# Streaming the columns of every split-precision matmul in a woven order, with staggered weight slots

## The chip, the cores and the metric

The kernel runs on one core of one Trainium2 chip, as one launch. The time is device microseconds (us) of that core. A profiled execution gives a trace beside it; its span is the time from the first to the last instruction.

## The reference, cut to what matters

The input is one sequence of 256 tokens of width 1024, in float32. Five stages follow one another on the residual stream h, each behind an RMS norm: a gated feed-forward block, a mixer (a linear recurrence, windowed attention, and their projections), a second feed-forward block, and two layers of another hybrid kind (a convolution, a low-rank attention, a dilated attention in three groups, and gated output products).

```python
def swiglu(x, w_gu, w_down):                       # D_FF = 2816
    g, u = jnp.split(x @ w_gu, 2, axis=-1)
    return (jax.nn.silu(g) * u) @ w_down
...
    h = x
    f = swiglu(rms_norm(h, ffn1_pre_g), ffn1_w_gu, ffn1_w_down)
    h = h + 0.5 * rms_norm(f, ffn1_post_g)
    m = hybrid_mixer(rms_norm(h, mix_pre_g), ...)    # z = u @ w_in, ..., merged @ w_out
    h = h + rms_norm(m, mix_post_g)
    f = swiglu(rms_norm(h, ffn2_pre_g), ffn2_w_gu, ffn2_w_down)
    h = h + 0.5 * rms_norm(f, ffn2_post_g)
    for l in range(2):
        h = hybrid_layer(h, ..., w_in_2[l], ..., w_o_2[l])   # proj = h @ w_in, ..., x + merged @ w_o
```

Nearly all of the arithmetic is products of the 256 tokens with weight matrices that are read from HBM once, 227 MB in all.

## The kernel before, in words

Every large product is done in split precision. A float32 operand is written as the sum of two numbers of the type fp32r, hi and lo, and a product of two operands is three matmuls that add up in one PSUM tile: hi by hi, hi by lo, lo by hi. That is `mm3` (lines 221 to 225; its three matmuls are lines 223, 224 and 225, and all big groups of the trace carry these lines). A matmul holds a stationary operand of 128x128, which a weight load (PEld in the profile) puts into the array, and streams the columns of a moving operand past it.

The activations lie transposed in two tiles, xh and xl, of 8 x 256 columns (8 groups of 128 features, 256 tokens each). Weights come in units: `unit` starts one transfer into a slot of pool `raw` (four slots), and `split_raw` makes hi from it by a copy on ScalarE (line 206) and lo by a subtraction on VectorE (line 207), both in one slot of pool `w`. Pool w has NW = 8 slots of 8192 bytes in each partition, used in turn; hi and lo of a unit lie in one slot. A few units at the end of a stage go to slots of other pools (w2, b4, s) so that they can be loaded ahead.

There are two ways round in which a product uses them:

- `stepA`, `down` and `out_proj`: the tokens are the stationary operand (128 of them by 128 features) and the weights move, 512, 416 or 384 columns at a time. These are the groups ga, ua, q, kv, c, dqk, uq, ukv, dn and o.
- `pairB`: 128 columns of weights are the stationary operand and the 256 tokens move. These are gu, gp, xg, g, bz, cx, zb and po.

A feed-forward block walks over 11 pairs of 256 hidden columns: gu products of one pair, then the dn products of the pair before; the units of the last three pairs lie in pool w2, and their dn products come at the end. Mixer and layers run such products while small jobs (transposes, attention scores, values) are let in between the matmuls by `tick`, which keeps its own account of time.

The pools lie in each partition in the order of their making: constants, raw, w, small tiles, then b4, n, t, then xh and xl, then the pools of the stage. `softplus` (called once, from `params`, during the first feed-forward block) makes eight constants of 32 bytes, of which two are needed later; pool `t` is a turning pool of four scratch slots that the activations of the gu products use as well.

Of the kernel before, what the change touches and what calls it, by code (L numbers as in the profile page):

```python
# [10 lines left out]
F32 = mybir.dt.float32  # L11
F32R = mybir.dt.float32r
# [4 lines left out]
P = 128  # L17
# [4 lines left out]
NW = 8  # L22
# [60 lines left out]
CW = CONST.shape[1] - 512  # L83


def rows(x):
    return lambda k: (x[0][:, k], x[1][:, k])


class Job:  # L90
# [3 lines left out]
    def __init__(self, gen, ready):  # L94
        self.gen, self.ready, self.done = gen, ready, False


class Kern:
    def __init__(self, tc, a, ex):
        self.tc, self.nc, self.a = tc, tc.nc, a  # L100
        pool = lambda name, bufs, **kw: ex.enter_context(tc.tile_pool(name=name, bufs=bufs, **kw))
        self.const = pool("const", 1)
        self.rawp = pool("raw", NRAW)
        self.wp = pool("w", NW)
        self.sm = pool("sm", 6)
        self.pools = {n: pool(n, k) for n, k in (("b4", NB4), ("n", NN), ("t", NT))}
        self.xp = pool("xT", 1)
        self.psum = pool("ps", 1, space=PSUM)
        self.now, self.live, self.last = 0.0, 0, None
        self.taken = deque([-W_X] * NX)  # L110
        self.lanes = {n: deque() for n in ("tp", "T", "S")}

# [85 lines left out]
    def split_raw(self, raw, kt, cols, pool="w"):  # L198
        nc = self.nc
        if pool in ("w", "w2"):  # L200
            p = self.wp if pool == "w" else self.pools[pool]
            w = p.tile([P, 2, kt, cols], F32R, tag=pool, name=pool)
            hi, lo = w[:, 0], w[:, 1]
        else:
            hi, lo = (self.tl(pool, [P, kt, cols], "w" + pool, F32R) for _ in range(2))
        nc.scalar.copy(hi, raw)  # L206
        nc.vector.tensor_tensor(lo, raw, hi, op=ALU.subtract)  # L207
        return hi, lo
# [11 lines left out]

    def mm3(self, out, ah, al, bh, bl, first, last):
        m = self.nc.tensor.matmul
        m(out, lhsT=ah, rhs=bh, start=first, stop=False)  # L223
        m(out, lhsT=ah, rhs=bl, start=False, stop=False)  # L224
        self.last = m(out, lhsT=al, rhs=bh, start=False, stop=last).ins  # L225
# [104 lines left out]
    def softplus(self):  # L330

        nc = self.nc
        T = lambda n: self.const.tile([P, 8], F32, name=n)
        ts, tt, stt = nc.vector.tensor_scalar, nc.vector.tensor_tensor, nc.vector.scalar_tensor_tensor
        neg, absl, t, e, z, z2, s = (T(f"sp{i}") for i in range(7))
        ts(neg, self.lam, -1.0, None, op0=ALU.mult)
        tt(absl, neg, self.lam, op=ALU.max)
        nc.scalar.activation(t, absl, AF.Tanh, scale=1.0 / 32)
        ts(z, t, 1.0, None, op0=ALU.add)
        nc.vector.reciprocal(z, z)  # L340
        ts(e, t, -1.0, 1.0, op0=ALU.mult, op1=ALU.add)
        tt(e, e, z, op=ALU.mult)
        for _ in range(4):
            tt(e, e, e, op=ALU.mult)
        ts(z, e, 2.0, None, op0=ALU.add)
        nc.vector.reciprocal(z, z)
        tt(z, e, z, op=ALU.mult)
        tt(z2, z, z, op=ALU.mult)
        nc.vector.memset(s, 1.0 / 17)
        for n in (15, 13, 11, 9, 7, 5, 3, 1):  # L350
            tt(s, s, z2, op=ALU.mult)
            ts(s, s, 1.0 / n, None, op0=ALU.add)
        tt(s, s, z, op=ALU.mult)
        ts(neg, neg, 0.0, None, op0=ALU.max)
        self.sp2, self.nsp4 = T("sp2"), T("nsp4")
        ts(s, s, 4.0, None, op0=ALU.mult)
        stt(self.sp2, in0=neg, scalar=2.0, in1=s, op0=ALU.mult, op1=ALU.add)
        ts(self.nsp4, self.sp2, -2.0, None, op0=ALU.mult)
# [128 lines left out]
    def transposed(self, parts, take, name, rows=P):  # L487

        yield from self.room()
        ps = self.bank("x", name, (P, len(parts), P))  # L490
        for i, x in enumerate(parts):
            self.nc.tensor.transpose(ps[0:rows, i], x, self.id)
        take(ps[0:rows])
        yield 0.107 * len(parts), W_TP
# [73 lines left out]
    def mixer(self, xT):  # L568
# [37 lines left out]
        def gate(c0, f, th):  # L606
            col = c0 + f * 512
            banks = self.pairB(rows(xT), [w[:, col:col + 256], w[:, col + 256:col + 512]], "g", tags=("accB", "accB"))
            for j in range(2):
                nc.scalar.activation(th[j], banks[j], AF.Tanh, scale=0.5)  # L610
# [100 lines left out]
    def heads(self, pairs, v, mask, scale, emit, deps, out, sinks=None):  # L711
# [39 lines left out]
        def values():  # L751
            for m in range(len(pairs)):
                while len(ready) <= m or self.now < ready[m][1]:
                    yield 0.0, 0.3
                s = ready[m][0]
                yp = self.bank("yp", "yT", (P, S))
                pts = []
                for j in range(2):
                    yield from self.room()
                    pts.append(self.prob_T([s[:, j, b * P:(b + 1) * P] for b in range(3)]))  # L760
                    yield 0.32, W_T
                self.live -= 1
                self.pv_pair(yp, v[m], pts, True, True)
                emit(m, yp)
                yield 1.1, 0.0

        self.spawn("S", scores())
        out.append(self.spawn("T", values()))

# [420 lines left out]
class DilPair:  # L1190
# [46 lines left out]
    def attend(self, sz, yc, out):  # L1237
# [6 lines left out]
        def scores():  # L1244
            yield from k.after(*self.jobs)
            mx, nm, rs = (k.small([P, 2, 2], x) for x in ("dmx", "dnm", "drs"))
            sm = k.small([P, 2, 2, 3], "dsm")
            ss = []
            for g in range(3):
                s = yield from k.s_tile(2)  # L1250
                ss.append(s)
                yield from k.room(2)
                ps = k.score_pair([(qd[r, g], kd[r, g]) for r in rows])
                for j in range(2):
                    for t, c, dc in sides:
                        nc.vector.tensor_tensor_reduce(
                            s[:, j, c], in0=ps[j][:, c], in1=k.dist[:, g, dc], scale=-SLOPES[8 * g + 2 * m + j],
                            scalar=-3e38 if g == 0 else mx[:, j, t:t + 1], op0=ALU.add, op1=ALU.max, accum_out=mx[:, j, t:t + 1])
                yield 1.1, W_SC
            nc.vector.tensor_scalar(nm, mx, -1.0, None, op0=ALU.mult)  # L1260
            for g, s in enumerate(ss):
                for j in range(2):
                    for t, c, _ in sides:
                        nc.scalar.activation(s[:, j, c], s[:, j, c], AF.Exp, bias=nm[:, j, t:t + 1], accum_out=sm[:, j, t, g:g + 1])
            nc.vector.tensor_reduce(rs, sm, axis=mybir.AxisListType.X, op=ALU.add)
            nc.vector.reciprocal(rs, rs)
            for s in ss:
                for j in range(2):
                    for t, c, _ in sides:
                        nc.vector.tensor_scalar(s[:, j, c], s[:, j, c], rs[:, j, t:t + 1], None, op0=ALU.mult)  # L1270
            ready.append((ss, k.now + W_SD))

        def values():
            if not yc:
                yc.extend([k.b4([P, 4, S], "ych", F32R), k.b4([P, 4, S], "ycl", F32R)])
            while not ready or k.now < ready[0][1]:
                yield 0.0, 0.3
            yp = k.bank("yp", "dyT", (P, S))
            for g, s in enumerate(ready[0][0]):
                pts = []  # L1280
                for j in range(2):
                    yield from k.room()
                    pts.append(k.prob_T([s[:, j, b * P:(b + 1) * P] for b in range(3)]))
                    yield 0.32, W_T
                k.live -= 1
                k.pv_pair(yp, [[vd[:, b, (2 * g + j) * 64:(2 * g + j + 1) * 64] for b in range(2)] for j in range(2)], pts, g == 0, g == 2)
                yield 1.1, 0.0
            k.gated(yc, sz, m, yp)
            yield 0.64, 0.0

        k.spawn("S", scores())
        out.append(k.spawn("T", values()))

# [32 lines left out]
```

## Time and profile before

| | |
|---|---|
| time, median of 2 runs | 1368.24 us (1367.99 to 1368.49) |
| profiled execution | 1368.98 us |
| its span | 1367.2 us |
| PE, weight loads, VectorE, ScalarE busy | 98%, 90%, 69%, 57% of the span |
| read from HBM | 227.64 MB, 167 GB/s over the span with what is written |

The spans of matmuls in the trace overlap: a matmul's end is modelled, so its pace is read from the distance between the starts of neighbours, not from its duration.

### The profile page before, as it was taken

To read this page: it belongs to the slowest core of one execution; us is meant where nothing else is said; L and a number is where in the kernel's file an instruction comes from. 1 tells how busy PE (TensorE), PEld (TensorE's weight loads), DVE (VectorE), ACT (ScalarE), POOL (GpSimd) and SP (SyncE) were. 2 spreads that over 40 slices of the span, in tenths; PEclk is the share of its full clock that TensorE was granted. 3 is DMA by queue.
4 is the path that set the end of the run, shared out by engine and by line. 5 is a ranking of instruction groups with operands and counts; after the bars stand their busy time and mean duration, and the time that the engine had idled before them with its cause. 6 is when DMAs were issued, how large, how long until landed. Compare 5 with 4: busy or idle time off the path is not lost.

```text
span 1367.2 us, 24721 instructions
## 1 busy us (share of the span) xinstructions
PE 1339.2 (98%) x9434; PEld 1236.1 (90%) x9434; DVE 950.1 (69%) x2178; ACT 780.5 (57%) x1464; POOL 3.0 (0%) x10
## 2 busy tenths in 40 slices
PE   7999999999999999999999999999999999999998
PEld 5999987888998899998998989999889989899997
DVE  6546667887878655558888676665788886766663
ACT  6444544787754544444667776454546667755451
POOL 0000000000000000000000000000000000000000
PEclk9999999999999999999999999999999999999999
DMA  7657764436565565673754454656556553556661
GB/s 257 220 165 226 227 210 150 122 115 156 166 207 183 176 192 186 201 229 86 218 139 123 129 170 124 184 172 187 174 160 176 150 133 96 174 157 178 186 183 49
DMA packets 234807, 230.30 MB, mean 168 GB/s; under 512 B 12336, under 2 KB 213184, under 8 KB 234688
## 3 DMA queue, kind: packets, MB, share of 16 engines
q1 hardware_dynamic: 232432, 227.05, 55.7%
q10 hardware_dynamic: 2256, 1.67, 0.5%
q8 instruction: 74, 1.21, 0.4%
q14 instruction: 45, 0.37, 0.1%
HBM read 227.64 MB, written 1.05 MB: 167 GB/s over the span
## 4 chain that ended last, share of the span: by engine, by line
PE 83%; DVE 8%; ACT 4%; DMA 3%; issue 2%; SPq 0%; ACTq 0%; DVEq 0%
PE gu L225 5%; PE gu L223 5%; PE gu L224 5%; PE dqk L223 4%; PE dqk L225 4%; PE dqk L224 4%; PE gp L223 3%; PE gp L225 3%; PE gp L224 3%; PE dn L223 3%; PE dn L225 3%; PE dn L224 3%; PE po L223 2%; PE po L225 2%; PE po L224 2%; PE sc L791 2%
## 5 line engine op out<-in xcount | busy, mean ns | idle before, releaser
L207 DVE TENSOR_TENSOR w<-raw,w 128x1024 fp32r<-128x1024 f32 (+1 forms) x437 | 502.4, 1157 | 234.1 <-ACT w L206 232.4
L206 ACT CAST w<-raw 128x1024 fp32r<-128x1024 f32 (+1 forms) x437 | 432.8, 999 | 348.6 <-PE gu L225 53.6
L223 PE MATMUL gu<-xh,w 128*128 128x256 f32 x576 | 161.4, 280 | 0.0
L225 PE MATMUL gu<-xh,w 128*128 128x256 f32 x576 | 161.1, 280 | 0.0
L224 PE MATMUL gu<-xl,w 128*128 128x256 f32 x576 | 160.7, 279 | 0.0
L223 PE MATMUL dqk<-w,xh 128*128 128x384 f32 x384 | 136.7, 356 | 3.0 <-ACT sq L1023 3.0
L224 PE MATMUL dqk<-w,xh 128*128 128x384 f32 x384 | 129.7, 338 | 0.0
L225 PE MATMUL dqk<-w,xl 128*128 128x384 f32 x384 | 129.3, 337 | 0.0
L223 PE MATMUL gp<-xh,w 128*128 128x256 f32 x384 | 109.2, 285 | 0.0
L224 PEld LDWEIGHTS gu<-xl,w 128*128 128x128 f32 x576 | 108.0, 188 | 0.7
L223 PEld LDWEIGHTS gu<-xh,w 128*128 128x128 f32 x576 | 107.9, 187 | 0.7
L225 PEld LDWEIGHTS gu<-xh,w 128*128 128x128 f32 x576 | 108.2, 188 | 0.0
L224 PE MATMUL gp<-xl,w 128*128 128x256 f32 x384 | 107.2, 279 | 0.0
L225 PE MATMUL gp<-xh,w 128*128 128x256 f32 x384 | 107.1, 280 | 0.0
L223 PEld LDWEIGHTS dqk<-w,xh 128*128 128x128 f32 x384 | 72.1, 188 | 9.9 <-issue 6.0
L223 PEld LDWEIGHTS gp<-xh,w 128*128 128x128 f32 x384 | 72.0, 187 | 3.1 <-issue 2.7
L224 PEld LDWEIGHTS dqk<-w,xh 128*128 128x128 f32 x384 | 72.3, 188 | 0.2
L224 PEld LDWEIGHTS gp<-xl,w 128*128 128x128 f32 x384 | 72.2, 188 | 0.0
L225 PEld LDWEIGHTS dqk<-w,xl 128*128 128x128 f32 x384 | 72.1, 188 | 0.0
L225 PEld LDWEIGHTS gp<-xh,w 128*128 128x128 f32 x384 | 71.9, 188 | 0.0
L223 PE MATMUL dn<-w,aT 128*128 128x512 f32 x176 | 69.2, 393 | 0.0
L224 PE MATMUL dn<-w,aT 128*128 128x512 f32 x176 | 69.2, 393 | 0.0
(377 smaller groups left out, 3245.8 us busy)
## 6 DMA issues: line engine op xcount, KB each, us to landing
raw<-in_w_in_dram SPq DMA_DIRECT2D x140, 512.0 KB
raw<-in_ffn_w_gu_dram SPq DMA_DIRECT2D x88, 512.0 KB
raw<-in_w_in_dram SPq DMA_DIRECT2D x192, 192.0 KB
raw<-in_ffn_w_down_dram SPq DMA_DIRECT2D x44, 512.0 KB
raw<-in_w_o_dram SPq DMA_DIRECT2D x16, 512.0 KB
raw<-in_w_proj_attn_dram SPq DMA_DIRECT2D x16, 256.0 KB
raw<-in_w_proj_lru_dram SPq DMA_DIRECT2D x8, 512.0 KB
raw<-in_w_out_dram SPq DMA_DIRECT2D x8, 512.0 KB
```

The source lines that it names most:

```text
L206: nc.scalar.copy(hi, raw)
L207: nc.vector.tensor_tensor(lo, raw, hi, op=ALU.subtract)
L223: m(out, lhsT=ah, rhs=bh, start=first, stop=False)
L224: m(out, lhsT=ah, rhs=bl, start=False, stop=False)
L225: self.last = m(out, lhsT=al, rhs=bh, start=False, stop=last).ins
L791: self.nc.tensor.matmul(p[:, c], lhsT=q[:, cq], rhs=k[:, ck], start=True, stop=True)
```

## The change

`mm3` rearranges the moving operand and the output alike. Where the number of columns is a multiple of 128 (256, 384 and 512; not 416), the columns are taken 16 of the first half, 16 of the second half, the next 16 of the first half, and so on. Each column of the output still gets the product of its own column, so the tiles hold what they held before; only the order of streaming differs. Pool w gets one slot of its own name for each of the eight places, in the same rotation, with a tile of 64 bytes behind each slot that nothing uses; a slot is thus 8256 bytes from the next, and the eight begin 64 bytes apart mod 512. To have room, the seven scratch tiles of softplus become parts of one tile of pool t, and its two results get names of their own.

```diff
+def weave(x):
+    return x if x.shape[1] % 128 else x.rearrange("p (h a c) -> p a h c", h=2, c=16)
...
-        self.wp = pool("w", NW)
+        self.wp = pool("w", 1)
+        self.nw = 0
...
         if pool in ("w", "w2"):
-            p = self.wp if pool == "w" else self.pools[pool]
-            w = p.tile([P, 2, kt, cols], F32R, tag=pool, name=pool)
+            if pool == "w":
+                i = self.nw % NW
+                w = self.wp.tile([P, 2, kt, cols], F32R, tag=f"w{i}", name="w")
+                if self.nw < NW:
+                    self.wp.tile([P, 16], F32, tag=f"pad{i}", name=f"pad{i}")
+                self.nw += 1
+            else:
+                w = self.pools[pool].tile([P, 2, kt, cols], F32R, tag=pool, name=pool)
...
     def mm3(self, out, ah, al, bh, bl, first, last):
         m = self.nc.tensor.matmul
+        out, bh, bl = weave(out), weave(bh), weave(bl)
         m(out, lhsT=ah, rhs=bh, start=first, stop=False)
...
     def softplus(self):
         nc = self.nc
-        T = lambda n: self.const.tile([P, 8], F32, name=n)
+        scr = self.t([P, 7, 8], "sp")
+        T = lambda n: scr[:, int(n[2])] if n[2:].isdigit() else self.const.tile([P, 8], F32, name=n)
...
-        self.sp2, self.nsp4 = T("sp2"), T("nsp4")
+        self.sp2, self.nsp4 = T("spp"), T("nsp")
```

## Rows read from the trace of the kernel before

**Rows 1.** The page: busy time of each engine, and the chain by engine.
```profile
PE 1339.2 (98%) x9434; PEld 1236.1 (90%) x9434; DVE 950.1 (69%) x2178; ACT 780.5 (57%) x1464; POOL 3.0 (0%) x10
...
PE 83%; DVE 8%; ACT 4%; DMA 3%; issue 2%; SPq 0%; ACTq 0%; DVEq 0%
```

**Rows 2.** Windows: length, PE, PEld, DVE, ACT, POOL busy, clock, DMA share, GB/s.
```profile
0.00:50.00 50.00, 39.81 (x213) 33.00 (x214) 32.97 (x55) 29.31 (x40) 0.70 (x6) 1.00 0.80 261
...
241.00:463.00 222.00, 216.44 (x1589) 196.19 (x1588) 176.46 (x385) 152.11 (x293) 1.27 (x2) 1.00 0.51 154
```

**Rows 3.** Timeline of PE (start, duration), gate-up products; 20 rows left out.
```profile
104.05 0.28 PE L223 MATMUL gu<-xh,w 128*128 128x256 f32 x1
...
106.52 0.28 PE L223 MATMUL gu<-xh,w 128*128 128x256 f32 x1
```

**Rows 4.** Timeline of the weight loads at the same place.
```profile
104.05 0.19 PEld L224 LDWEIGHTS gu<-xl,w 128*128 128x128 f32 x1
```

**Rows 5.** Timeline of PE, gate products of the mixer, two stretches.
```profile
290.54 0.28 PE L224 MATMUL g<-xl,w 128*128 128x256 f32 x1
...
292.35 0.28 PE L225 MATMUL g<-xh,w 128*128 128x256 f32 x1
...
293.78 0.28 PE L224 MATMUL g<-xl,w 128*128 128x256 f32 x1
...
294.96 0.28 PE L225 MATMUL g<-xh,w 128*128 128x256 f32 x1
```

**Rows 6.** Windows of these two stretches, columns as in rows 2.
```profile
290.54:292.35 1.81, 1.81 (x18) 1.81 (x17) 1.24 (x2) 1.30 (x4) 0.00 (x0) 1.00 1.04 348
293.78:294.96 1.18, 1.18 (x13) 1.18 (x11) 1.18 (x4) 1.18 (x4) 0.00 (x0) 1.00 0.88 305
```

**Rows 7.** Timeline of PE, the end of the first down product.
```profile
192.00 0.39 PE L225 MATMUL dn<-w,aT 128*128 128x512 f32 x1
...
194.34 0.39 PE L223 MATMUL dn<-w,aT 128*128 128x512 f32 x1
194.56 0.40 PE L224 MATMUL dn<-w,aT 128*128 128x512 f32 x1
...
202.29 0.39 PE L225 MATMUL dn<-w,aT 128*128 128x512 f32 x1
```

**Rows 8.** Timeline of PE, products of 384 columns; 8 rows left out between.
```profile
653.84 0.34 PE L225 MATMUL dqk<-w,xl 128*128 128x384 f32 x1
...
655.40 0.34 PE L225 MATMUL dqk<-w,xl 128*128 128x384 f32 x1
```

**Rows 9.** Groups by line and shape: count, busy us, mean ns of one.
```profile
L224 PE MATMUL gu<-xl,w 128*128 128x256 f32 x576 | 160.7, 279 | 0.0
L224 PE MATMUL dqk<-w,xh 128*128 128x384 f32 x384 | 129.7, 338 | 0.0
L224 PE MATMUL gp<-xl,w 128*128 128x256 f32 x384 | 107.2, 279 | 0.0
L224 PE MATMUL dn<-w,aT 128*128 128x512 f32 x176 | 69.2, 393 | 0.0
L224 PE MATMUL bz<-xl,w 128*128 128x256 f32 x128 | 35.7, 279 | 0.0
L224 PE MATMUL o<-w,mT 128*128 128x512 f32 x60 | 23.7, 394 | 0.0
L224 PE MATMUL po<-yal,w 128*128 128x256 f32 x64 | 17.9, 280 | 0.0
L224 PE MATMUL ga<-w,xh 128*128 128x512 f32 x32 | 13.5, 421 | 0.6 <-DVE w L207 0.6
L224 PE MATMUL o<-wb,mT 128*128 128x512 f32 x28 | 10.9, 391 | 0.0
L837 PE MATMUL lg<-xc,wab 128*128 128x256 f32 x16 | 4.8, 383 | 0.0
```

**Rows 10.** Timeline of VectorE, the last instruction of softplus.
```profile
117.46 0.17 DVE L358 TENSOR_SCALAR nsp<-sp 128x8 f32<-128x8 f32 x1
```

## The prediction

> **What bounds the kernel now.** Read the page's busy shares first, then its chain [rows 1]. PE is busy 1339.2 of the span's 1367.2 us, and 83% of the chain that ended last lies on it. VectorE works 69% and ScalarE 57% of the time, and in no stage are they the bound: even in the mixer, where VectorE works most, it has 176 us of work in 222 us [rows 2]. Only the first 50 us differ: there the DMA engines are 0.80 busy and PE waits for weights, so a faster matmul gains nothing in them.
>
> A busy PE may still run below its rate, so the next view is the order of time, and in it the distance from one start to the next (the durations of the rows overlap and say little). In the gate-up products 21 steps of 256 columns take 2.47 us, 117.6 ns each [rows 3]. The granted clock is 1.00, that is 2.4 GHz, in every stretch [rows 2, 6], and 256 columns at 2.4 GHz are 106.7 ns. So 11 ns, or 10%, of each such product is something else. Each weight load starts with the product ahead of its own [rows 3, 4], so one reader fetches 128 columns of a stationary operand while another streams the moving one.
>
> Two pairs of rows show what the 11 ns depend on. First, the same line with the same operands runs at 113.1 ns a step from 290.54 us (16 steps in 1.81 us) and, after a few transposes, at 118.0 ns from 293.78 us (10 steps in 1.18 us) [rows 5]. The shapes and the addresses mod 512 are the same; only the moment at which the stream was entered differs, and each pace then holds. VectorE and ScalarE are busy in both stretches, longer in the slow one [rows 6]; but the gate-up stretch [rows 3] and the slow one agree to 0.4 ns. Second, in the down product 10 steps from 192.00 us take 234.0 ns each and 34 steps from 194.56 us 227.4 ns [rows 7]. The second stretch streams units of pool w2 and the first those of pool w. The sizes of the pools, added up in their order, put the w slots at 256 mod 512 bytes and w2, aT, xh and xl at 64. The output product shows it again within one stage: its moving units from the slots take 394 ns, those from pool b4 391 [rows 9]. So a product is slower by 4.5 to 6.6 ns in some relations of the place where the moving operand is read to the place where the weights are read, and I read this as the two readers meeting in the same place, a place being 64 bytes mod 512. This reading is an inference; the paces are measured.
>
> Take the fast pace as a floor: 113.1 ns is 6.4 ns above 106.7, over 16 runs of 64 bytes 0.40 ns a run. At 512 columns it is 227.4 less 213.3 over 32 runs, 0.44 ns, so the floor goes with the columns and is no cost of the weight load, of which there is one in each case.
>
> **What the Trainium skill says of it.** In "TensorE: Matmul & The Clock Gate", Part 2, step-by-step, it says that PE has two independent read ports and that loading the next weights takes no bandwidth from the running matmul. By that rule the change would be worth nothing (third rival); the two paces of one product [rows 5] speak against it.
>
> **The change part by part.**
> *The order of the columns.* Plain, the moving reader passes 512 bytes twice in 256 columns. If the weights' reader passes its 512 bytes about once in that time, the faster reader overtakes it, once a load. Woven, the moving reader takes 16 columns of one half and then 16 of the other; for 256 and 512 columns the halves lie 512 and 1024 bytes apart, the same place mod 512, so it walks the 512 bytes at half the pace. If both then walk alike, a pair that does not start together never meets. That the weights' reader has this pace is no row; its load takes 188 ns [rows 4] with its fixed part in it. What a meeting costs, by size:
> 256 columns: 117.6 less 113.1, 4.5 ns. Per line there are 576 gu, 384 gp, five groups of 128 (bz stands for cx, zb, xg and g) and five of 64 (po), that is 1920, times three lines 5760 [rows 9]: 25.9 us.
> 384 columns: 9 steps in 1.56 us are 173.3 ns [rows 8], the floor is 1.5 times 113.1, 169.7: 3.6 ns. 384 dqk [rows 9] and 16 of uq, times three, are 1200: 4.3 us. Their halves lie 768 bytes apart, so here two relations of eight would be bad, not one.
> 512 columns: 234.0 less 227.4, 6.6 ns. dn, o, ga, ua, q and 24 of kv and ukv make 392 a line, 1176 [rows 9]; of these 144 of dn (three of its eleven pairs of units) and 108 of o are not in w slots and run at the floor already, so 924 count: 6.1 us. The 96 products of 416 columns are not woven.
> Together 36.3 us. The 192 products of ga and ua in the first 50 us fall away (1.3 us): 35.0.
> *The places of the slots.* Eight tiles of 32 bytes leave the constants and two stay, 192 bytes less; eight pads of 64 bytes come in. So the slots begin at 64, 128, ... 448 and 0 mod 512, and all that lies behind them, xh, xl, aT and w2, at 384. Of eight slots one begins with the operand that it meets and could keep the meeting, or all of it: I count 7/8, 30.6 us; 6/8 (a neighbour spoiled as well) and 8/8 are the ends.
> *What is left of it in the span.* Splits, evictions and norms keep their lengths. PE idles 28.0 us by the busy row, and its waits at the ends of stages do not shrink. Where VectorE has 79% of a stage, some of the gain turns into waits for split weights. I take 95%, ends 85% and 100%: 29.1 us. Nothing is late next on the whole: VectorE in the mixer would go from 79% to 81%.
> *Softplus scratch.* The seven small tiles become one slot of pool t. The same VectorE instructions run, the last at 117.46 us [rows 10]. The slot is asked for again four tiles later, which is two pairs of gate-up banks, each 17 us or more after the allocation near 100.7 us, when softplus is over. Cost: nothing; if that order failed, an activation of one pair would wait, and PE behind it, some microseconds once. No wait, DMA or instruction is added elsewhere, and the pads are never written.
>
> The profiled execution took 1368.98 us, 1.8 above its span and 0.7 above the median 1368.24. Off the median: 1368.24 - 29.1 = 1339. The ends of the unknown shares (36.3 us; 35.0 x 6/8 x 0.85 = 22.3) give 1332 to 1346.
>
> **What no row prices: the jump itself.** All products of the trace read and write plain runs. The nearest row for a run's price is the floor's own 0.40 ns. From below: if it is paid because the next 64 bytes lie in another place, the woven order pays it for every second run, and gains. From above: a jump could cost it once more at each run, or a product could lose its rate of one column a cycle, which a row shows too: the plain fp32 product of 256 columns takes 383 ns where gu takes 279 [rows 9], 104 ns more, 599 us over the 5760. I take nothing, being nearest to the paces of 0.40 ns a run, which a jump at a run's border need not change.
> The Trainium skill, "SBUF — State Buffer", Door 1, its box on cachelines, says that PSUM has lines of 8 bytes and that any non-contiguous PSUM pattern slows matmuls significantly. It speaks against the change, whose output jumps every 64 bytes; no row has such an output. Taken at its word it makes the second rival below the result.
>
> **The rivals.**
> 1. The run's price falls too. For 256 columns 8 of 16 runs save 0.40 ns, 3.2 ns, 18.4 us over 5760; for 512 columns 6.4 ns, 7.5 us over 1176. With the forecast's 29 that is 55 us: 1313; if all the price went (63.5 us, next item), 1276. For it: the floor goes with the runs. Against: nothing in the rows says that it is a matter of place.
> 2. Jumps cost. One more 0.40 ns a run is 6.4 ns x 5760 = 36.9, 9.6 ns x 1200 = 11.5 and 12.8 ns x 1176 = 15.1 us, 63.5 together, on PE in every stage. With meetings avoided, 1403; with them kept, 1432; with the rate lost, over 1900. It decides from 29.1/63.5 of 0.40 ns, 0.18 ns a run: above that the kernel is slower than before. For it: output and input both jump. Against: the jumps fall on borders of 64 bytes, where the rows show a price already.
> 3. It does not do what it says: the readers' paces are other than I take them, so that the woven stream meets the weights as often as the plain one: 1368, with up to 10 us either way.
>
> **How the numbers follow.** Forecast 0.50, rival 1 0.17, rival 2 0.23, rival 3 0.10. A difference under 2% (1341 to 1396) counts as none here. The forecast's ends straddle 1341: 0.29 of it is faster, 0.21 within. Rival 1 is faster, rival 3 within, of rival 2 0.03 within. So faster 0.46, same 0.34, slower 0.20. The range 1300 to 1405 takes in the forecast with its ends, rival 3, most of rival 1 and the mild half of rival 2; about 0.18 is left out.
>
> **What would show it.** In the forecast the gate-up steps are near 113 ns in seven slots of eight, those of the down product near 227 in all pools, and a slower slot comes back every eighth unit. Rival 1: steps of 110 ns or less. Rival 2: 120 ns or more in all slots alike. Rival 3: 118 as now. Wrong altogether would be an even pace that has nothing to do with the slot, or PE gaps before products of w that are not there now.

## The result and the profile after

The changed kernel takes 1406.4 us (1404.8 to 1408.01, 2 runs) against 1368.24: 1.0277 times the time before, with a 95% interval of 1.0256 to 1.0298. It is slower by 38 us where 29 us less were forecast. The profiled execution took 1408.01 us, its span 1406.2.

The page of the changed kernel, busy shares and the chain by engine, answers to [rows 1]:

```profile
PE 1373.3 (98%) x9434; PEld 1262.4 (90%) x9434; DVE 952.6 (68%) x2178; ACT 781.5 (56%) x1464; POOL 3.0 (0%) x10
...
PE 77%; DVE 8%; DMA 7%; ACT 5%; issue 2%; SPq 0%; ACTq 0%; DVEq 0%
```

PE has 34 us more work with as many instructions, and PE's share of the chain went down while DMA's rose from 3% to 7%. So two things happened: the matmuls became slower, and somewhere PE now waits for transfers. The timeline of PE shows both (start us, duration us, instruction):

```profile
107.11 0.28 PE L240 MATMUL gu<-xh,w 128*128 128x256 f32 x1
...
109.88 0.28 PE L239 MATMUL gu<-xl,w 128*128 128x256 f32 x1
...
180.23 0.28 PE L240 MATMUL gu<-xh,w 128*128 128x256 f32 x1
180.35 0.40 PE L238 MATMUL dn<-w,aT 128*128 128x512 f32 x1
...
191.63 0.40 PE L240 MATMUL dn<-w,aT 128*128 128x512 f32 x1
197.48 0.58 PE L238 MATMUL gu<-xh,w 128*128 128x256 f32 x1 [5.45 <-ACT w L220]
...
206.19 0.28 PE L240 MATMUL gu<-xh,w 128*128 128x256 f32 x1
206.40 0.51 PE L238 MATMUL dn<-w,aT 128*128 128x512 f32 x1
...
206.98 0.40 PE L240 MATMUL dn<-w,aT 128*128 128x512 f32 x1
...
211.30 0.40 PE L238 MATMUL dn<-w,aT 128*128 128x512 f32 x1
...
312.17 0.28 PE L239 MATMUL g<-xl,w 128*128 128x256 f32 x1
...
313.37 0.28 PE L240 MATMUL g<-xh,w 128*128 128x256 f32 x1
...
671.32 0.34 PE L239 MATMUL dqk<-w,xh 128*128 128x384 f32 x1
...
674.92 0.34 PE L238 MATMUL dqk<-w,xh 128*128 128x384 f32 x1
```

*The pace.* 23 gate-up steps in 2.77 us are 120.4 ns, where [rows 3] had 117.6; 10 gate steps in 1.20 us are 120.0, where [rows 5] had 113.1 and 118.0; 18 down steps in 4.32 us are 240.0 where [rows 7] had 227.4 for the same units of pool w2; 20 steps of 384 columns in 3.60 us are 180.0, where [rows 8] had 173.3. Each is 18 cycles of 2.4 GHz for 16 columns. Over the whole trace the mean at 256 columns is 120.0 to 120.3 ns in each of the eight slots: no good slots and no bad one. Multiplied out against the means of before (117.7, 174.7 and 232.1 ns): 5760 x 2.4, 1200 x 5.5 and 1176 x 8.1 ns are 30 of PE's 34 us.

*The wait.* In the kernel before, all 288 gate-up products of the last three pairs come first and then the 96 last down products:

```profile
180.44 0.28 PE L225 MATMUL gu<-xh,w 128*128 128x256 f32 x1
180.56 0.39 PE L223 MATMUL dn<-w,aT 128*128 128x512 f32 x1
```

Now 240 come, then 48 down products, then PE stands until 197.48 us, and the last 48 gate-up products follow among the rest of the down products. A window on that place shows what comes with it (length, busy us of PE, PEld, DVE, ACT and POOL, granted clock, DMA share, GB/s):

```profile
195.00:205.00 10.00, 7.52 (x42) 7.14 (x43) 4.63 (x4) 5.03 (x5) 0.00 (x0) 0.66 0.79 247
```

The granted clock falls to its lower level, 1.2 GHz, while PE stands, and is there for some 7 of the 10 us (0.66 in the mean). PE works in it from 197.48 us on, and the 2 us or so that this costs are half of the 4 us of its work that the pace leaves over.

### The profile page after: what moved, and what is told of

It reads as the page before. It is cut to its first block, busy times and chain, and to the rows that moved or that the text cites. A ratio compares the mean times of both kernels' runs of the same rounds, so it can differ in the third digit from the quotient of the medians.

```text
span 1406.2 us, 24750 instructions
## 1 busy us (share of the span) xinstructions
PE 1373.3 (98%) x9434; PEld 1262.4 (90%) x9434; DVE 952.6 (68%) x2178; ACT 781.5 (56%) x1464; POOL 3.0 (0%) x10
## 4 chain that ended last, share of the span: by engine, by line
PE 77%; DVE 8%; DMA 7%; ACT 5%; issue 2%; SPq 0%; ACTq 0%; DVEq 0%
PE dqk L238 4%; PE dqk L240 4%; PE dqk L239 4%; PE gu L238 4%; PE gu L240 4%; PE gu L239 4%; PE gp L238 3%; PE gp L240 3%; PE gp L239 3%; DMA raw<-in_w_in_dram 3%; DVE w L221 3%; ACT w L220 2%; PE sc L807 2%; PE po L238 2%; PE po L240 2%; PE po L239 2%
## 5 line engine op out<-in xcount | busy, mean ns | idle before, releaser
L221 DVE TENSOR_TENSOR w<-raw,w 128x1024 fp32r<-128x1024 f32 (+2 forms) x437 | 502.4, 1157 | 270.3 <-ACT w L220 269.0
L220 ACT CAST w<-raw 128x1024 fp32r<-128x1024 f32 (+2 forms) x437 | 432.4, 998 | 383.9 <-PE gu L240 64.0
L238 PE MATMUL gu<-xh,w 128*128 128x256 f32 x576 | 164.2, 285 | 5.9 <-ACT w L220 5.9
L240 PE MATMUL gu<-xh,w 128*128 128x256 f32 x576 | 163.3, 284 | 0.2 <-DVE w L221 0.2
L238 PE MATMUL dqk<-w,xh 128*128 128x384 f32 x384 | 139.2, 362 | 2.2 <-ACT sq L1039 2.2
L239 PE MATMUL dqk<-w,xh 128*128 128x384 f32 x384 | 132.1, 344 | 0.0
L238 PEld LDWEIGHTS gu<-xh,w 128*128 128x128 f32 x576 | 110.1, 191 | 7.6 <-ACT w L220 6.8
L238 PE MATMUL gp<-xh,w 128*128 128x256 f32 x384 | 110.8, 289 | 0.0
L240 PEld LDWEIGHTS gu<-xh,w 128*128 128x128 f32 x576 | 109.4, 190 | 0.7 <-DVE w L221 0.6
L240 PE MATMUL gp<-xh,w 128*128 128x256 f32 x384 | 108.5, 284 | 0.0
L238 PE MATMUL dn<-w,aT 128*128 128x512 f32 x176 | 71.5, 407 | 0.0
L239 PE MATMUL dn<-w,aT 128*128 128x512 f32 x176 | 71.1, 404 | 0.0
```

## The experiments

Each is a change to the kernel before unless it says otherwise. Its runs were made beside new runs of the kernel before on the same chip, which lay at 1369.5 to 1370.2 us. Runs of 8, 32 and 64 columns, the orders of one side and the two other orders have one run each. Steps are of gate-up products (256 columns) where nothing else is said.

**The parts of the change, alone.** The first has only the woven order (with `weave` as in the change):

```diff
+        out, bh, bl = weave(out), weave(bh), weave(bl)
```

> The kernel before with the woven order alone; pool w, its slots and softplus as before. Theory (the jumps cost: a run of 16 columns takes 18 cycles of 2.4 GHz where the plain order's best is 17): steps of 120 ns at 256 columns, 180 at 384, 240 at 512, whatever the slot; the time is 1368 + 5760 x 2.4 ns + 1200 x 5.5 ns + 1176 x 8.1 ns = 1398 us, and the wait of PE for weights near 195 us is gone. Rival (the places of the slots slow it, the order is neutral or a gain): steps of 113 to 118 ns, 1340 to 1368 us.

The second is the changed kernel without that line:

> The changed kernel with the plain order of columns: slots of their own names in strict turn, pads and softplus scratch stay. Theory (strict turn makes transfers wait for a slot that is still held while another is free): PE's wait and the drop of the granted clock near 195 us stay, 4 to 12 us are lost to them; what the places do to the pace shows by slot: 113 to 118 ns at 256 columns; 1360 to 1380 us. Rival (all of the slowdown is the order): 1368 us within 2 us, no wait near 195 us.

The third has the same places in plain order, but lets the pool give the slots:

```diff
+            if pool == "w":
+                w = self.wp.tile([P, 2 * kt * cols + 16], F32R, tag="w", name="w")
+                w = w[:, 0:2 * kt * cols].rearrange("p (a k c) -> p a k c", a=2, k=kt)
...
```

> The kernel before, plain order, with slots of 8256 bytes in one pool of eight buffers: the same eight places 64 bytes apart, but the pool gives whichever slot comes free. Theory (readers that meet cost the plain order 4 to 7 ns, by the relation of places): steps differ by slot between 113 and 118 ns at 256 columns and 227 to 236 at 512, and the time is 1345 to 1368 us, without the wait near 195 us. Rival (the pace has nothing to do with the places): 118 ns in all slots, 1368 us.

The fourth is the third and the woven order:

> As the one before with the woven order: the whole change but for the strict turn of the slots. Theory: 120, 180 and 240 ns as in the changed kernel, but no wait near 195 us: 1398 us, some 9 below the changed kernel. Rival (the strict turn costs nothing): 1406 us.

| | us | ratio to before (95%) |
|---|---|---|
| woven order alone | 1392.13 | 1.0161 (1.0130 to 1.0193) |
| slots in strict turn, plain order | 1382.39 | 1.0090 (1.0059 to 1.0122) |
| same places, slots as they come free | 1368.65 | 0.9986 (0.9971 to 1.0002) |
| the last with the woven order | 1394.06 | 1.0176 (1.0140 to 1.0213) |

So the order costs 23 us and the strict turn 13, together 36 of the 38; that slots lie 64 bytes apart costs nothing by itself. Against what was expected, the two woven kernels lie 4 to 6 us below 1398, the third is just above its 1345 to 1368, and the strict turn is 2 us above its 1360 to 1380. The timeline of the woven order alone, 40 steps in 4.80 us, has 120.0 ns with all slots in their old place:

```profile
104.18 0.28 PE L232 MATMUL gu<-xh,w 128*128 128x256 f32 x1
...
108.98 0.28 PE L230 MATMUL gu<-xh,w 128*128 128x256 f32 x1
```

The page has 29 us more busy time for PE there, close to the 30 expected of the pace, but the time rose by 23:

```profile
PE 1368.5 (98%) x9434; PEld 1261.4 (91%) x9434; DVE 951.9 (68%) x2178; ACT 781.8 (56%) x1464; POOL 3.0 (0%) x10
```

PE's idle time fell from 28.0 to 22.3 us (span 1390.8): with slower products, PE's waits for results of VectorE and ScalarE in the mixer and the layers are shorter (for lGG in the g products 0.4 us where it was 2.4, for sq in dqk 1.7 where it was 3.0).

The third kernel shows how the plain order depends on the places. Its timeline, 21 steps in 2.38 us with weights in the slot at 64 mod 512, then 21 in 2.52 us in the slot at 128, moving operand at 384 in both (the trace holds no addresses; the slots are reckoned from the program):

```profile
128.79 0.28 PE L228 MATMUL gu<-xh,w 128*128 128x256 f32 x1
...
131.17 0.28 PE L228 MATMUL gu<-xh,w 128*128 128x256 f32 x1
...
148.41 0.28 PE L228 MATMUL gu<-xh,w 128*128 128x256 f32 x1
...
150.93 0.28 PE L228 MATMUL gu<-xh,w 128*128 128x256 f32 x1
```

113.3 ns in the one and 120.0 in the other, each held through its unit; over the trace the means of single units go from 113.3 to 120.0 ns. With the same slots in woven order all 240 units lie between 119.8 and 121.0.

The distance of the two operands is not all, though. In the second kernel the turn is strict, so the slot of a unit can be counted: the first unit of the ninth pair lies at 448 mod 512 and takes 23 steps in 2.71 us, 117.8 ns; the units in the slot at 64 take 117.6 to 117.9 in the first feed-forward block after their first one (115.1).

```profile
148.44 0.28 PE L237 MATMUL gu<-xh,w 128*128 128x256 f32 x1
...
151.15 0.28 PE L239 MATMUL gu<-xh,w 128*128 128x256 f32 x1
```

So one distance, that of the slot at 64, has shown both 113.3 and 117.8 ns, as one product did in [rows 5].

**Why the woven order is slow: which side, and which runs.** Weaving one side alone gives the work and the stalls of that side, with columns in the wrong places of the output.

```diff
+        bh, bl = weave(bh), weave(bl)
```

in the one kernel, and in the other

```diff
+        out = weave(out)
```

> The kernel before with only the moving operand woven and the output plain, so the columns of each product land in another order and the output is not the reference's; the work is the same. Theory (the price of a jump lies on the reading side): 120 ns steps at 256 columns, 240 at 512, about 1392 us. Rival (it lies on the PSUM side, as the Trainium skill's rule on non-contiguous PSUM patterns in SBUF - State Buffer, Door 1, would have it): 113 to 118 ns, about 1345 to 1368 us.

> The counterpart: only the output woven, the moving operand plain; the output is not the reference's. Theory (reading side): 113 to 118 ns at 256 columns and 227 to 236 at 512 as before, 1368 us. Rival (PSUM side): 120 and 240 ns, 1392 us.

The timeline with the moving operand woven, 40 steps in 4.80 us:

```profile
101.96 0.28 PE L232 MATMUL gu<-xh,w 128*128 128x256 f32 x1
...
106.76 0.28 PE L230 MATMUL gu<-xh,w 128*128 128x256 f32 x1
```

and with the output woven, 40 steps in 4.71 us:

```profile
103.05 0.28 PE L232 MATMUL gu<-xh,w 128*128 128x256 f32 x1
...
107.76 0.28 PE L230 MATMUL gu<-xh,w 128*128 128x256 f32 x1
```

120.0 ns and 1392.68 us in the one, 117.8 ns and 1369.17 us in the other (one run each; before 1370.19). The whole price is paid where the moving operand is read from SBUF. An output that jumps every 64 bytes in PSUM is free, so the Trainium skill's sentence in "SBUF — State Buffer", Door 1, that any non-contiguous PSUM pattern slows matmuls significantly, does not hold for runs of 64 bytes here.

Then the length of the runs, 64, 8 and 32 columns in place of 16 (`c=64`, `c=8`, `c=32` in `weave`):

> Input and output woven in runs of 64 columns instead of 16 (384 columns in runs of 64 as well). Theory (each jump costs one cycle of 0.42 ns beside the 17 cycles per 16 columns): 4 jumps in 256 columns, 115 ns if no readers meet and up to 120 if they do; 8 in 512, 230 to 237; 1350 to 1372 us. Rival (a woven stream is slowed as such, whatever the length of its runs): 120 and 240 ns, 1392 us.

> Runs of 8 columns, 32 bytes. Theory (one more cycle for each jump): 32 jumps in 256 columns, 256 + 16 + 32 = 304 cycles or 127 ns, 8 ns above the runs of 16; if the border of 64 bytes is paid on each return as well, 133 ns; 1430 to 1465 us. Rival (the price goes with the bytes read, not with the jumps): 120 ns, 1392 us.

> The kernel before with input and output woven in runs of 32 columns (128 bytes). Runs of 64 were free and runs of 16 cost 18 cycles for 16 columns, so a price for each jump is ruled out. Theory (what is short is a run of less than 128 bytes or so: reading goes ahead by more than 64 bytes, and a run that ends sooner loses a cycle): 113 to 118 ns at 256 columns, 1368 us. Rival (the price falls off steadily with the length of the run): half of the price of runs of 16, near 118.5 ns without the bimodal paces of the plain order, about 1380 us.

The timeline with runs of 64, 40 gate-up steps in 4.71 us and 25 gate steps in 2.83 us, and that with runs of 8, 40 steps in 4.93 us:

```profile
100.14 0.28 PE L232 MATMUL gu<-xh,w 128*128 128x256 f32 x1
...
104.85 0.28 PE L230 MATMUL gu<-xh,w 128*128 128x256 f32 x1
...
298.90 0.28 PE L231 MATMUL g<-xl,w 128*128 128x256 f32 x1
...
301.73 0.28 PE L232 MATMUL g<-xh,w 128*128 128x256 f32 x1
```

```profile
103.40 0.29 PE L232 MATMUL gu<-xh,w 128*128 128x256 f32 x1
...
108.33 0.29 PE L230 MATMUL gu<-xh,w 128*128 128x256 f32 x1
```

| run, columns | 64 | 32 | 16 | 8 |
|---|---|---|---|---|
| step at 256 columns, mean of the trace, ns | 117.6 | 118.8 | 120.0 | 123.3 |
| at 512 columns | 232.1 | 236.6 | 240.0 | 243.3 |
| time, us | 1368.71 | 1379.82 | 1392.13 | 1415.43 |

Runs of 64 columns change nothing, though the stream jumps four times in each product. Their mean of 117.6 ns does not settle it, since a cycle for each jump allowed 115 to 120; the gate steps do: 113.3 ns, the best pace of the plain order, where four cycles would make 115. So a jump after 64 columns is free. The same theory expected 127 to 133 ns for runs of 8 and is refuted by 123.3. For runs of 32 my theory missed (113 to 118 ns, 1368 us) and the rival held (half of the price of runs of 16, about 1380 us). The price grows as the runs get shorter. By what law can't be said: at 256 columns it is 1.1, 2.3 and 5.6 ns for runs of 32, 16 and 8 against the mean before, 5.5, 6.7 and 10.0 against the best pace, and the runs don't show which of the two to take.

Last, runs of 16 in other orders: from four quarters in turn (`h=4`), and first the even and then the odd runs (`"p (a h c) -> p h a c"`), so that nothing alternates.

> Runs of 16 columns from four quarters in turn instead of two halves: at 256 columns the next run lies 256 bytes on instead of 512. Theory (short runs pay, wherever the next lies): 120, 180 and 240 ns as with two halves, 1392 us. Rival (the next run in the same place mod 512 is what pays): 113 to 118 ns at 256 columns, where the step is no longer 512 bytes, 240 still at 512 columns, where it is; about 1365 to 1375 us.

> Runs of 16 columns again, but first all even runs and then all odd ones, so that one region is read upwards in steps of 128 bytes and no two regions alternate. Theory (short runs pay, wherever the next lies): 120 ns at 256 columns, 240 at 512, 1392 us. Rival (the alternation between regions pays): 113 to 118 ns and 227 to 236 ns, about 1368 us.

The timeline of the even-odd order, 40 steps in 4.82 us:

```profile
102.40 0.28 PE L232 MATMUL gu<-xh,w 128*128 128x256 f32 x1
...
107.22 0.28 PE L230 MATMUL gu<-xh,w 128*128 128x256 f32 x1
```

120.5 ns, 1391.99 us: reading upwards in runs of 64 bytes with 64 bytes left out costs as much as alternating between halves. So alternation is not what pays, and shortness is enough. The four quarters agree with neither expectation: 118.8 ns at 256 columns, 182.3 at 384, 235.6 at 512, 1381.48 us. Where the next run lies does matter in part; how is left open.

**The distance of the places.** Two small changes to the kernel before, in plain order: the softplus scratch alone, which shifts slots and the rest alike, and 128 unused bytes behind pool w, which shift the rest against the slots.

```diff
+        pool("gap", 1).tile([P, 32], F32, tag="gap", name="gap")
         self.sm = pool("sm", 6)
```

> The kernel before with the softplus scratch alone: no weave, no pads, eight buffers as before. It moves the w slots to 64 and all behind them to 384 mod 512, so that their distance stays as in the kernel before (192 bytes) at other places. Theory (the pace follows the distance alone): 117.7 ns at 256 columns, 1368 us. Rival (the places themselves count; with slots staggered the slot at 64 took 114.9 ns on average): 114.9 ns, 16 us less PE work, about 1354 us.

> The kernel before with 128 unused bytes behind pool w: slots stay at 256, all behind them goes to 192 mod 512, a distance that took 115.4 ns at 256 columns and 230.9 at 512 in the staggered run. Theory (the pace follows the distance): 5760 x 2.3 ns + 924 x 2.4 ns = 15 us less PE work, about 1354 us. Rival (the mix of paces is set by how each stream is entered): 117 to 118 ns, 1364 to 1370 us.

The shift of all gave 1369.73 us, ratio 0.9997 (0.9988 to 1.0007), 117.4 ns: places count only against one another. The gap gave 1353.67 us, ratio 0.9876 (0.9857 to 0.9895), as the theory said. Its timeline, 40 steps in 4.55 us, and its page:

```profile
101.58 0.29 PE L226 MATMUL gu<-xh,w 128*128 128x256 f32 x1
...
106.13 0.28 PE L224 MATMUL gu<-xh,w 128*128 128x256 f32 x1
```

```profile
PE 1320.0 (98%) x9434; PEld 1219.4 (90%) x9434; DVE 950.5 (70%) x2178; ACT 780.0 (58%) x1464; POOL 3.0 (0%) x10
```

113.8 ns a step (114.5 over the trace; 173.3 and 229.0 at 384 and 512 columns) and 19 us less busy time for PE, of which 16 are seen in the time. This kernel beats both: one line, no instruction more or fewer. Unit by unit (24 products each), 169 of its 240 units of 256 columns run at 113 to 114 ns and 39 at 118, where 231 of 240 ran at 118 before. Its distance is that of the slot at 448 above, which took 117.8 ns. So shifting the operands against each other changes how often the fast pace is met, and distance alone does not fix it; what else does is open. It is not the other engines: in the kernel before, units keep 117.7 to 117.8 ns with the DMA engines 0.33 busy (from 129.70 to 132.50 us) and 1.00 busy (169.30 to 172.00), and 29 steps between 100 and 190 us with VectorE and ScalarE both idle have 117.8 ns like the 508 others.

**The strict turn.** Two down units of the eighth pair, the last whose units go to pool w, are loaded early and used at the very end of a block (`p > NP - FFN_TAIL` sends only later pairs to w2; the down products of four pairs come at the end, not of three). Here the tail is cut to the pairs in w2, with strict turn and, as control, in the kernel before.

```diff
-FFN_TAIL = 4
+FFN_TAIL = 3
-            ... "w2" if p > NP - FFN_TAIL else "w")
+            ... "w2" if p >= NP - FFN_TAIL else "w")
```

> The slots in strict turn with the plain order, and the tail of the feed-forward blocks cut to the three pairs whose down units lie in pool w2, so that no unit of pool w is held until the end of a block. Theory (strict turn loses because the two units of the fourth pair from the end keep their slots until the last down products, and the turn runs into them): the last 48 gate-up products come before the last down products again, PE's wait near 190 us is gone, 1366 to 1374 us. Rival (strict turn loses everywhere a little): 1380 us or more.

> The control for it: the kernel before with the same shorter tail. Theory: with slots given as they come free nothing was lost there, so 1366 to 1374 us. Rival (the shorter tail is itself a gain or a loss): outside of that.

With strict turn 1377.0 us, ratio 1.0052 (1.0037 to 1.0067), the control 1371.66, ratio 1.0014 (1.0002 to 1.0027). In the windows from 50 to 241 us of three kernels, strict turn, the same places given as they come free, and strict turn with the shorter tail (columns as above), PE's busy time and clock tell the wait:

```profile
50.00:241.00 191.00, 185.54 (x1186) 166.85 (x1185) 115.68 (x206) 86.06 (x125) 1.26 (x2) 0.99 0.57 183
```

```profile
50.00:241.00 191.00, 190.32 (x1226) 171.58 (x1225) 122.04 (x216) 90.06 (x129) 0.98 (x2) 1.00 0.61 196
```

```profile
50.00:241.00 191.00, 190.32 (x1219) 171.64 (x1218) 119.84 (x211) 90.25 (x129) 0.99 (x2) 1.00 0.60 193
```

The wait is gone and the last gate-up products come before the last down products again, as the theory said. But only 5.4 of the 13 us came back (7.5 if the control's own loss is allowed for); I had expected 1366 to 1374. The traces show where the rest lies. At the end of the second feed-forward block this kernel and the control are level: the next transposes start at 626.82 and 626.75 us. One layer on they start at 1002.12 and 996.82. In between, PE waits for VectorE and ScalarE until 630.62 (1.34 us) and until 657.34 us (2.68; in the control 1.26 and 1.27), and in the stretches behind these waits the granted clock is at 1.2 GHz:

```profile
631.40:634.80 3.40, 3.40 (x12) 3.23 (x11) 3.40 (x15) 0.47 (x1) 0.00 (x0) 0.50 0.15 44
658.70:662.10 3.40, 3.40 (x12) 3.40 (x11) 2.17 (x7) 2.13 (x3) 0.00 (x0) 0.50 0.61 182
```

In the control it is 1.00 from 631.40 to 634.80 as well as from 654.40 to 657.80 us. At half speed 6.8 us lose 3.4, the longer waits 1.5. So the shorter tail gives back the loss in the feed-forward blocks, and the trace of the strict turn then loses some 5 us at the entry of the first layer; why its wait is longer there is open.

## Why the prediction was wrong, point by point

*What bounds the kernel, and the two paces.* Right: PE's rate sets the time, and the plain order's pace depends on where the two operands lie. The gap of 128 bytes shows it, with the time. That two readers meet in one place of 64 bytes mod 512 stays an inference, and the distance alone does not give the pace: the slot at 448 has the gap's distance and ran at 117.8 ns. The Trainium skill's independent ports ("TensorE: Matmul & The Clock Gate", Part 2) would have given the kernel with the gap the pace of the kernel before; it runs at 114.5 ns over the trace and not at 117.7. Two readings slipped, without weight for the result. In the first 50 us PE waits 9.4 us for the first normalised tokens and 0.6 for weights. And of the 192 products of ga and ua only half lie there; the others begin the second feed-forward block.

*The order of the columns, 36.3 us of gain.* No slot shows a gain. The woven stream has neither good nor bad slots, as an order that never meets would, but at a pace above all but the worst of the plain ones. Whether the meetings are avoided or hidden under the longer reading can't be told from these runs.

*The jump itself, "I take nothing".* This is the step that failed. From the floor of 113.1 ns the woven runs cost 6.9 ns at 256 columns, 10.3 at 384 and 12.6 at 512: 39.7 + 12.4 + 14.8 = 67 us. Rival 2 had sized it at 63.5 us, from the 0.40 ns a run that the floor itself shows, and its sign, 120 ns or more in all slots alike, is what the trace has. Counted from the floor its size was right and its cause was not: a jump after 64 columns is free, and what costs is that a run is short, on the reading side alone. That its time, 1403 with the meetings gone, lies near 1406 is luck in part: the order alone gave 1392, and 13 us come from the strict turn, which rival 2 leaves out. My reason for taking nothing, that the jumps fall on borders where a price is already paid, was no evidence for a price of zero; the even-odd order, whose jumps fall on the same borders, pays in full.

*The places of the slots, 7/8.* No slot is spoiled or spared in the woven order; the term has no counterpart. In the plain order staggering the slots is neutral, since fast and slow units average out: 117.4 ns over the trace against 117.7.

*No wait or DMA added.* Wrong, by 13 us. I took the eight named slots for the same rotation, and the account of the change says so too. The pool of eight buffers did not turn strictly: it passed over slots still held, and gave the free ones. The two held units are followed by eight gate-up units in pool w, and the last two of these ran before the held ones were used (180.44 us above), which a strict turn does not allow. With names, each unit must wait for its own slot; where two units are held to the end of a feed-forward block, loads stop behind them, the last gate-up products slip behind down products, and PE idles 5.45 us and then runs on the lower clock. PE gaps that were not there before were one of the signs named for being wrong altogether.

*Softplus scratch.* Right: alone it gives 0.9997.

*What is left in the span.* 95% was forecast for a gain. For the woven order's loss it was 23 of 30 us, and for the gap's gain 16 of 24 us of summed steps. PE's idle time takes up part of the difference both ways: 5.7 us less of it in the one, 3.9 us more in the other (1351.9 less 1320.0 against 28.0). That term was too near to one.

## What to carry to other kernels

Where matmuls run back to back, compare the distance of their starts with columns over clock; if the same product has two paces, shift the pools of the stationary and the moving operand against each other and measure, as the distance alone does not tell the pace: here one unused tile of 128 bytes gave 1.2%. Stream the moving operand in runs of 64 columns of float32 or more; an output may be scattered in runs of 64 bytes. Before buffers of a pool are given names, look whether any of them is held for long, since names turn "whichever is free" into "this one".

## What the runs showed of the hardware that was not expected

An fp32r matmul at 2.4 GHz takes 17 cycles for 16 columns at its best in plain order (113.3 ns at 256, 226.7 at 512), 18 in woven runs of 16, and up to 18 in plain order in some slots (120.0 ns). Short runs of the moving operand in SBUF cost (123.3 ns with runs of 32 bytes, 120.0 with 64, 118.8 with 128, nothing with 256), short runs of the output in PSUM do not. The pace goes with the pair of operands, not with other engines: with VectorE and ScalarE both idle it is 117.8 ns as with them busy. One distance can show two paces (113.3 and 117.8 ns); what picks one of them no run here settles.
